# A hybrid decoder layer on one core: spills of y in four pieces, a second pool of slots, the diagonals of 1/rms earlier, and h of the second half on VectorE

## The chip, the core and the metric

The kernel runs on one core of a Trainium2 chip. The core has TensorE (PE in the profile; PEld is its weight load), VectorE (DVE), ScalarE (ACT), GpSimd (POOL) and SyncE (SP), which issues the transfers between memory and the on-chip SBUF. Matmuls write PSUM; VectorE and ScalarE read it, GpSimd doesn't. The metric is device time in microseconds (us) for one execution.

## The reference, cut to what matters

```
h = rmsnorm(x, g_pre) * (1 + scale) + shift        # x: 2048 tokens x 1024
proj = h @ w_in                                    # 7 groups of 512 columns
gu, gv, gg, rq, rk, rv, rg = split(proj)
y_gmlp = gu * (tril(w_s) LN(gv) + b) * silu(gg)    # 4 groups of 128 columns
y_ret = groupnorm(retention(rot(rq), rot(rk), rv)) * silu(rg)   # 4 heads of 128
y = concat(y_gmlp, y_ret)                          # 2048 x 1024
x + gate * rmsnorm(y @ w_out, g_post)
```

Everything is float32. `scale`, `shift` and `gate` come from a small matmul of `c` ahead of the rest.

## The kernel before, in words

**Tokens.** They are worked in two halves of 1024, each of two quads of 512 tokens. Activations lie transposed: 128 features in the partitions, tokens along the row. A tile of 128x512 float32 is 256 KB, 2 KB in each partition, and is the unit of nearly all work. Such tiles come from one pool, `big`, of 80 slots, handed out by `slot`; a new tile of it waits until the readers of the slot's last tile are done.

**Products.** A float32 product is three matmuls of 128x512 in a reduced format, high by high, low by high and high by low. Each operand is split for it: ScalarE writes the high part (`wh`, `hh`, `yh`), VectorE the rest (`wl`, `hl`, `yl`), one tile at a time.

**Stages of a half.** First the projections of v, q and k for retention (`token_unit`, 8 ticks of three matmuls for a chunk of 128 tokens), then v of the gMLP, then six *units* r0, r1, g0, u0, g1, u1 (numbers 0 to 5): two by two blocks of the gates and of u, each done with seven Strassen-Winograd products of four ticks instead of eight. VectorE adds the products up (`u`, `c`, line 783) out of PSUM, and the results multiply into y (`used`, lines 757 to 773): yR for retention, yT for the gMLP. y of a half is written to memory (`yspill`) and read back (`ya`) in the output stage at the end, which again pairs tokens for Strassen (`ys` are its sums) and multiplies by `w_out`, whose blocks are `or`. Weights of the units are loaded as `ur` and combined on GpSimd (`ut`).

**What sets the order.** PE, DVE, ACT and POOL run in the order in which the program emits the work, and `slots` is a hand-written timetable of it: `slots.at(t, fn)` puts a step t ticks ahead. `pump()` splits the next block of weights; how many run in each product of a unit is in EXTRA_PUMPS. SP's order is made by a scheduler from the same program.

**h of the second half.** `hbuild` makes the 16 tiles of h for tokens 1024 to 2047 (8 feature blocks, two quads) while the first half's units run. It needs `rb`, a row of 1/rms for each quad, spread over the partitions: `xdiag2` splits 4 columns of 1/rms (`rsh`, `rsl`) and makes eight 128x128 diagonals (`dgr`) on VectorE, and `xrow` multiplies them by ones on TensorE. BUILD tells at which tick of which unit this happens ("diag", "row", "x" for the load, "h" for a tile); the second quad's eight tiles are built from line 1139 on, where the second half's v projection starts (the *seam*).

Of the kernel before, what the change touches and what calls it, by code (L numbers as in the profile page):

```python
# [11 lines left out]
F32 = mybir.dt.float32  # L12
# [24 lines left out]
QK_PUMPS = ((), (), (1,), (1,), (1,), (1,), (1, 4), (1, 4))  # L37
EXTRA_PUMPS = {(0, 5): (0, 0, 0, 1, 1, 1, 2), (1, 4): (0, 1, 0, 1, 0, 1, 1), (1, 5): (0, 1, 1, 1, 1, 1, 1)}
SLOTS = 80
# [5 lines left out]
            ("B22", "S4"))  # L45
BUILD = {3: ((2, "diag", 0), (14, "row", 0), (20, "x", 0), (21, "x", 1)),
# [3 lines left out]
RV_PUMPS = ((1,),) * 7 + ((1, 4),)  # L50
# [48 lines left out]
def tile_hybrid_layer(ctx: ExitStack, tc, x, xt, wm, wg, win, wun, wout, wst, cols, rows, pos, cst,  # L99
# [39 lines left out]

    def slot(name, shape=(512,), dtype=F32):  # L140
        return big.tile([P, *shape], dtype, name=name, tag="s")


    raw, blocks = {}, {}
# [176 lines left out]
    def hnew(half, q, kb):  # L321
        hi, lo = slot("hh", dtype=F32R), slot("hl", dtype=F32R)
        hT[half, q, kb] = (hi, lo)
        return hi, lo
# [93 lines left out]
    def v_small(half, ch, ps, when=(0, 1, 7, 12, 14)):  # L418
# [28 lines left out]
        def into_y():  # L447
            y = yT[half, ch // QUAD]
            for g in range(GROUPS):
                V.scalar_tensor_tensor(y[:, ch % QUAD, g, :], box["mx"][:, g, :],  # L450
                                       cols_t[:, 32 + g:33 + g], bs_b[:, g, :], ALU.mult, ALU.add)
# [17 lines left out]
    def ret_pair(pool, half, pr_, ch, ps, delay=0):  # L469
# [99 lines left out]
        def into_y():  # L569
            for i in range(2):  # L570
                h = h0 + i
                S.activation(yR[half, ch // QUAD][:, :, h, :], box["ytp", i], AF.Copy,
                             scale=cols_t[:, 36 + h:37 + h])
# [10 lines left out]

    def yspill(half, part):
        for ch in range(NCH):
            t = yd[half, ch, part] = ydram.tile([P, 4, P], F32, name=f"yd{half}{ch}{part}")
            SP.dma_start(t, (yR, yT)[part][half, ch // QUAD][:, ch % QUAD, :, :])


    def pair_loads(half, ch):
        a = {}

        def load():
            for m in range(2):
                for part in range(2):
                    t = a[f"A{m + 1}{part + 1}"] = slot("ya", (4, P))
                    SP.dma_start(t, yd[half, ch + QUAD * m, part])

        return a, load  # L600
# [156 lines left out]
    def used(half, kind, pair, up, c, q, nj, in_psum):  # L757
        y = (yR if kind == "r" else yT)[half, q][:, :, 2 * pair + nj, :]
        c3 = c.rearrange("p (c t) -> p c t", c=QUAD)

        def times(eng, by):
            eng.tensor_tensor(y, y, by, ALU.mult)  # L762

        if kind == "u":
            slots.at(0, lambda: times(V if in_psum else G, c3))
            return

        def gate():
            g = up.tile([P, QUAD, P], F32, name="sg", tag="k", bufs=6) if in_psum else c3
            S.activation(g, c3, AF.Silu)  # L770
            slots.at(1, lambda: times(G, g))

        slots.at(0, gate)
# [317 lines left out]

    areas = []

    def opened(name):
        areas.append(tc.tile_pool(name=name, bufs=1, reuse_waits="tile"))
        return areas[-1].__enter__()

    def closed(n=1):
        for _ in range(n):
            areas.pop().__exit__(None, None, None)  # L1100

    def y_tiles(name, half, to):
        pool = opened(f"{name}{half}")
        for q in range(2):
            to[half, q] = pool.tile([P, QUAD, 4, P], F32, name=f"{name}{half}{q}")

# [11 lines left out]
    def build1(q, kb):  # L1118
        n = q * KB + kb
        hbuild(1, q, kb, hb["x"].pop(0), hb[q], kb % 2 == 1 if q else kb in (1, 7), (3, 5), True)  # L1120
        if n + 2 < 2 * KB:
            fetch1(n + 2)

    qk = {}
    for half in range(2):

        if half == 0:
            with tc.tile_pool(name="start", bufs=1, reuse_waits="tile") as sp:
                first = start(sp)
            y_tiles("yR", half, yR)  # L1130
            rp = opened(f"ret{half}")
# [4 lines left out]
        for ch in range(QUAD if half == 0 else 0, NCH):  # L1136
            if half == 1 and ch == 0:
                for n in range(KB):
                    slots.at(6 + 3 * n, partial(build1, 1, n))
                slots.at(4, partial(yspill, 0, 1))  # L1140
            ps = token_unit(half, 0, ch, "prv", () if half == 0 else RV_PUMPS[ch])
            rv_small(half, ch, ps)
            if half == 1 and ch == 2:
                closed(3)
                y_tiles("yR", half, yR)
                rp = opened(f"ret{half}")
                for n, fn in enumerate(tables(half, rp)):
                    slots.at(n + 2, fn)
# [20 lines left out]
        for ch in range(NCH):  # L1169
            if ch == 2:  # L1170
                closed()
                y_tiles("yT", half, yT)
                up = opened(f"unit{half}")
# [9 lines left out]
        for un in range(len(UNITS)):  # L1183
# [3 lines left out]
            if un == 2:  # L1187
                slots.at(4, partial(yspill, half, 0))
            if half == 0 and un in BUILD:
# [12 lines left out]

    slots.at(3, partial(yspill, 1, 1))
    pools = []
# [75 lines left out]
```

## Time and profile before

| | |
|---|---|
| median of 3 runs | 907.1 us (906.3 to 907.86) |
| the profiled execution | 906.63 us, span 904.9 us |
| TensorE busy | 850.8 us (94%) |
| VectorE busy | 663.7 us (73%) |
| GpSimd busy | 415.5 us (46%) |
| ScalarE busy | 319.8 us (35%) |
| transfers | 100.60 MB, mean 111 GB/s |

The span is from the first to the last instruction; 1.7 us of the execution lie around it. Busy shares are averages over stages with different limits. The granted clock of TensorE is given as a share of 2.4 GHz, so 0.50 is 1.2 GHz.

### The profile page before, as it was taken

To read this page: it belongs to the slowest core of one execution; us is meant where nothing else is said; L and a number is where in the kernel's file an instruction comes from. 1 tells how busy PE (TensorE), PEld (TensorE's weight loads), DVE (VectorE), ACT (ScalarE), POOL (GpSimd) and SP (SyncE) were. 2 spreads that over 40 slices of the span, in tenths; PEclk is the share of its full clock that TensorE was granted. 3 is DMA by queue.
4 is the path that set the end of the run, shared out by engine and by line. 5 is a ranking of instruction groups with operands and counts; after the bars stand their busy time and mean duration, and the time that the engine had idled before them with its cause. 6 is when DMAs were issued, how large, how long until landed. Compare 5 with 4: busy or idle time off the path is not lost.

```text
span 904.9 us, 11859 instructions
## 1 busy us (share of the span) xinstructions
PE 850.8 (94%) x4074; PEld 698.6 (77%) x4074; DVE 663.7 (73%) x1242; ACT 319.8 (35%) x621; POOL 415.5 (46%) x448
## 2 busy tenths in 40 slices
PE   2999999999999995999999999999999968899996
PEld 1778888888888884777888888888888746678885
DVE  4989876567984648779886665897356797887776
ACT  4673223323453334451111221354423343433341
POOL 2040363355756556130334334675548663545451
PEclk9999999999999998999999999999999979999999
DMA  8961331300021422463232100011331844364432
GB/s 324 330 238 37 92 117 59 103 14 1 8 87 47 163 70 70 129 231 129 81 94 94 59 1 1 1 47 47 138 83 49 291 149 177 112 222 178 140 141 93
DMA packets 49597, 100.60 MB, mean 111 GB/s; under 512 B 5888, under 2 KB 6016, under 8 KB 49536
## 3 DMA queue, kind: packets, MB, share of 16 engines
q1 hardware_dynamic: 49536, 99.83, 32.9%
q8 instruction: 32, 0.52, 0.2%
q14 instruction: 29, 0.24, 0.1%
HBM read 83.03 MB, written 16.78 MB: 110 GB/s over the span
## 4 chain that ended last, share of the span: by engine, by line
PE 77%; DVE 10%; DMA 6%; issue 4%; ACT 2%; POOL 1%; SPq 0%; DVEq 0%; ACTq 0%; POOLq 0%
PE pqk L241 6%; PE pqk L239 6%; PE pqk L240 5%; PE pY L241 3%; PE pY L239 3%; PE pY L240 3%; PE pv L241 3%; PE pv L240 3%; PE pv L239 3%; DVE wl L187 2%; PE pX L239 2%; PE pX L240 2%; PE pX L241 2%; PE pZ L239 2%; PE pZ L241 2%
## 5 line engine op out<-in xcount | busy, mean ns | idle before, releaser
L239 PE MATMUL pqk<-wh,hh 128*128 128x512 f32 x240 | 102.3, 426 | 0.0
L502 POOL TENSOR_TENSOR rA<-rA,rB 128x512 f32<-128x512 f32 x32 | 42.5, 1327 | 118.9 <-DVE rB L494 84.8
L241 PE MATMUL pqk<-wh,hl 128*128 128x512 f32 x240 | 94.7, 395 | 0.0
L240 PE MATMUL pqk<-wl,hh 128*128 128x512 f32 x240 | 93.7, 390 | 0.0
L516 ACT COPY qkT<-tp 128x512 f32<-128x512 f32 x32 | 18.8, 586 | 155.6 <-PE tp L507 155.6
L187 DVE TENSOR_TENSOR wl<-wr,wh 128x512 fp32r<-128x512 f32 x62 | 63.9, 1045 | 1.9 <-ACT wh L184 1.7
L762 POOL TENSOR_TENSOR yT<-yT,c 128x512 f32<-128x512 f32 x24 | 37.2, 1556 | 60.7 <-DVE c L783 43.0
L241 PEld LDWEIGHTS pqk<-wh,hl 128*128 128x128 f32 x240 | 45.0, 188 | 10.4
L239 PE MATMUL pv<-wh,hh 128*128 128x512 f32 x128 | 51.9, 406 | 0.0
L240 PEld LDWEIGHTS pqk<-wl,hh 128*128 128x128 f32 x240 | 45.5, 189 | 6.8 <-issue 0.2
L239 PEld LDWEIGHTS pqk<-wh,hh 128*128 128x128 f32 x240 | 45.4, 189 | 6.4 <-issue 0.2
L241 PE MATMUL pv<-wh,hl 128*128 128x512 f32 x128 | 50.1, 391 | 0.0
L240 PE MATMUL pv<-wl,hh 128*128 128x512 f32 x128 | 50.0, 390 | 0.0
L783 DVE TENSOR_TENSOR u<-pY,s 128x512 f32<-128x512 f32 x24 | 16.5, 688 | 42.7 <-PE pY L241 25.3
L241 PE MATMUL pY<-sh,wl 128*128 128x512 f32 x96 | 38.6, 402 | 9.5 <-DVE wl L187 9.5
L184 ACT CAST wh<-ut 128x512 fp32r<-128x512 f32 x48 | 28.7, 620 | 47.7 <-POOL ut L224 47.6
L241 PE MATMUL zY<-wh,yl 128*128 128x512 f32 x96 | 38.4, 400 | 3.0 <-DVE yl L618 2.9
L439 ACT ACTIVATE vh<-pv,nbv,rsv 128x128 f32<-128x128 f32 x64 | 24.1, 456 | 47.4 <-POOL nbv L434 47.4
L560 DVE TENSOR_SCALAR yq<-o,gmv,grs 128x128 f32<-128x128 f32 x64 | 23.3, 405 | 23.8 <-POOL grs L553 23.8
L672 POOL TENSOR_SCALAR zrs<-zss 128x1 f32<-128x1 f32 x16 | 18.2, 1139 | 47.5 <-ACT jz L665 46.9
L239 PE MATMUL zY<-wh,yh 128*128 128x512 f32 x96 | 38.1, 397 | 2.0 <-DVE u L668 1.1
L492 DVE TENSOR_TENSOR rA<-pqk,cos_t 128x512 f32<-128x512 f32 x28 | 19.2, 687 | 28.1 <-PE pqk L241 28.1
(251 smaller groups left out, 2641.8 us busy)
## 6 DMA issues: line engine op xcount, KB each, us to landing
wr<-in_win SPq DMA_DIRECT2D x64, 256.0 KB, 3.5
ur<-in_wun SPq DMA_DIRECT2D x48, 256.0 KB, 3.1
slab<-in_wm SPq DMA_DIRECT2D x16, 512.0 KB, 6.4
ya<-yd SPq DMA_DIRECT2D x32, 256.0 KB, 3.9
xr<-in_x SPq DMA_DIRECT2D x16, 512.0 KB, 4.6
out<-xr SPq DMA_DIRECT2D x32, 256.0 KB, 2.2
or<-in_wout SPq DMA_DIRECT2D x28, 256.0 KB, 5.3
xt<-in_xt SPq DMA_DIRECT2D x24, 256.0 KB, 4.8
```

The costliest lines, as they stand in the source:

```text
L184: S.copy(hi, r)
L187: eng.tensor_tensor(lo, r, hi.bitcast(F32), ALU.subtract)
L239: T.matmul(ps, l[0], r[0], start=first, stop=False, skip_group_check=reopened)
L240: T.matmul(ps, l[0], r[1], start=False, stop=False, skip_group_check=reopened)
L241: T.matmul(ps, l[1], r[0], start=False, stop=last, skip_group_check=reopened)
L439: S.activation(vh[:, g, :], ps[:, g * P:(g + 1) * P], AF.Identity, bias=nb[:, g:g + 1], scale=rs[:, g:g + 1])
L492: V.tensor_tensor(A, ps.rearrange("p (g d) -> p g d", g=8), tab["cos"][:, ch, :].unsqueeze(1).broadcast_to([P, 8, 64]), ALU.mult)
L502: G.tensor_tensor(A, A, box["B"].rearrange("p g h d -> p (g h d)"), ALU.add)
L516: S.copy(qkT, box["tp"])
L560: V.tensor_scalar(yq[h][:, ch % QUAD, :], box["o"][:, i, :], mv[:, i, 0:1], rs[:, i:i + 1], ALU.subtract, ALU.mult)
L672: G.tensor_scalar(r, ss[:, m, 0:1], ss[:, m, 1:2], EPS, ALU.add, ALU.add)
L762: eng.tensor_tensor(y, y, by, ALU.mult)
```

## The change

1. EXTRA_PUMPS: in the second half four more blocks of weights are split in units 3 to 5, ahead of the output stage (35 for 31); in the first half the 19 of units 4 and 5 are spread otherwise.
2. BUILD: both diagonals and rows are made in unit 2 (they were in units 3 and 5), the eight h tiles of the first quad in units 3, 4 and 5 (they were in 4 and 5), and those of the second quad start at tick 1 of the seam, not 6.
3. `build1`: all 16 h tiles are built with two VectorE instructions and one ScalarE instruction. Ten of them took one GpSimd, two ScalarE and one VectorE instruction before.
4. y of a half is no longer one tile for a quad but eight tiles of 2 KB. yR of the first half has a pool of its own (`ys`, 8 slots), which the first four blocks of h of the second half then use; yR of the second half lies in `big`, which frees its slots after its spill.
5. `yspill` writes one column group (one head or group) of one quad with one transfer, 512 pieces of 512 bytes, where it wrote one chunk of 128 tokens in 128 pieces of 2 KB. The number of transfers stays. yT leaves in two pieces, columns 0 and 1 in unit 4, columns 2 and 3 at the end, where all of it left at the end.
6. `used`: the last unit of the second half multiplies three results into yT on VectorE, which did it on GpSimd.

```diff
@@ -35,7 +35,8 @@
 SUMS_G = ((), (), (0, 5), (4, 6), (5, 7), (5, 7), (), ())
 V_PUMPS = ((),) * 7 + ((1, 4),)
 QK_PUMPS = ((), (), (1,), (1,), (1,), (1,), (1, 4), (1, 4))
-EXTRA_PUMPS = {(0, 5): (0, 0, 0, 1, 1, 1, 2), (1, 4): (0, 1, 0, 1, 0, 1, 1), (1, 5): (0, 1, 1, 1, 1, 1, 1)}
+EXTRA_PUMPS = {(0, 4): (0, 0, 0, 0, 0, 1, 1), (0, 5): (0, 0, 0, 1, 0, 1, 1), (1, 3): (0, 0, 0, 1, 0, 1, 1),
+               (1, 4): (1, 1, 0, 1, 1, 1, 1), (1, 5): (1, 0, 1, 0, 1, 1, 1)}
 SLOTS = 80
 TOKEN_PASSES = 4
 R_WHEN = (0, 2, 5, 6, 8, 9, 10, 11, 12, 14, 15, 16)
@@ -43,10 +44,10 @@
 GROUP = {"u": 0, "g": 2, "r": 6}
 PRODUCTS = (("B11", "A11"), ("T2", "S2"), ("B21", "A12"), ("T3", "S3"), ("T1", "S1"), ("T4", "A22"),
             ("B22", "S4"))
-BUILD = {3: ((2, "diag", 0), (14, "row", 0), (20, "x", 0), (21, "x", 1)),
-         4: ((14, "h", 0, 0), (22, "h", 0, 1)),
-         5: ((0, "diag", 1), (3, "h", 0, 2), (7, "h", 0, 3), (11, "h", 0, 4), (14, "row", 1),
-             (15, "h", 0, 5), (19, "h", 0, 6), (23, "h", 0, 7))}
+BUILD = {2: ((1, "diag", 0), (8, "row", 0), (12, "diag", 1), (19, "row", 1), (20, "x", 0), (21, "x", 1)),
+         3: ((5, "h", 0, 0), (18, "h", 0, 1)),
+         4: ((3, "h", 0, 2), (12, "h", 0, 3), (21, "h", 0, 4)),
+         5: ((3, "h", 0, 5), (12, "h", 0, 6), (20, "h", 0, 7))}
 RV_PUMPS = ((1,),) * 7 + ((1, 4),)
 GROUPS_OUT = (2, 1, 1, 1, 1, 1, 1)
 EPS = 1e-6
@@ -137,9 +138,21 @@
     invf_b = const.tile([P, 64], F32, name="invf_b")
     tab = {}
 
-    def slot(name, shape=(512,), dtype=F32):
-        return big.tile([P, *shape], dtype, name=name, tag="s")
-
+    def slot(name, shape=(512,), dtype=F32, pool=None):
+        return (pool or big).tile([P, *shape], dtype, name=name, tag="s")
+
+
+    areas, opens = [], []
+
+    def opened(name, bufs=1):
+        opens.append(tc.tile_pool(name=name, bufs=bufs, reuse_waits="tile"))
+        areas.append(opens[-1].__enter__())
+        return areas[-1]
+
+    def closed(n=1):
+        for _ in range(n):
+            areas.pop()
+            opens.pop().__exit__(None, None, None)
 
     raw, blocks = {}, {}
     IN_BLOCKS = TOKEN_PASSES * KB
@@ -319,7 +332,8 @@
         return t
 
     def hnew(half, q, kb):
-        hi, lo = slot("hh", dtype=F32R), slot("hl", dtype=F32R)
+        pool = areas[0] if half == 1 and q == 0 and kb < 4 else None
+        hi, lo = slot("hh", dtype=F32R, pool=pool), slot("hl", dtype=F32R, pool=pool)
         hT[half, q, kb] = (hi, lo)
         return hi, lo
 
...
@@ -569,7 +583,9 @@
         def into_y():
             for i in range(2):
                 h = h0 + i
-                S.activation(yR[half, ch // QUAD][:, :, h, :], box["ytp", i], AF.Copy,
+                y = slot("yR", (QUAD, P), pool=None if half else areas[0])
+                yR.setdefault((half, ch // QUAD), {})[h] = y
+                S.activation(y, box["ytp", i], AF.Copy,
                              scale=cols_t[:, 36 + h:37 + h])
 
         steps = [rotate, added, turn, turned, score, causal, outp, stats, root, norm]
@@ -582,10 +598,12 @@
     ydram = ctx.enter_context(tc.tile_pool(name="ydram", bufs=1, space=bass.MemoryType.DRAM))
     yd = {}
 
-    def yspill(half, part):
-        for ch in range(NCH):
-            t = yd[half, ch, part] = ydram.tile([P, 4, P], F32, name=f"yd{half}{ch}{part}")
-            SP.dma_start(t, (yR, yT)[part][half, ch // QUAD][:, ch % QUAD, :, :])
+    def yspill(half, part, cols):
+        for q in range(2):
+            if (half, part, q) not in yd:
+                yd[half, part, q] = ydram.tile([P, QUAD, 4, P], F32, name=f"yd{half}{part}{q}")
+            for n in cols:
+                SP.dma_start(yd[half, part, q][:, :, n, :], (yR, yT)[part][half, q][n])
 
 
     def pair_loads(half, ch):
...
@@ -755,14 +773,14 @@
         return on_v, on_g, late
 
     def used(half, kind, pair, up, c, q, nj, in_psum):
-        y = (yR if kind == "r" else yT)[half, q][:, :, 2 * pair + nj, :]
+        y = (yR if kind == "r" else yT)[half, q][2 * pair + nj]
         c3 = c.rearrange("p (c t) -> p c t", c=QUAD)
 
         def times(eng, by):
             eng.tensor_tensor(y, y, by, ALU.mult)
 
         if kind == "u":
-            slots.at(0, lambda: times(V if in_psum else G, c3))
+            slots.at(0, lambda: times(V if in_psum or (half == 1 and pair == 1) else G, c3))
             return
 
         def gate():
...
@@ -1117,7 +1127,7 @@
 
     def build1(q, kb):
         n = q * KB + kb
-        hbuild(1, q, kb, hb["x"].pop(0), hb[q], kb % 2 == 1 if q else kb in (1, 7), (3, 5), True)
+        hbuild(1, q, kb, hb["x"].pop(0), hb[q], True, (3, 5))
         if n + 2 < 2 * KB:
             fetch1(n + 2)
 
@@ -1127,7 +1137,7 @@
         if half == 0:
             with tc.tile_pool(name="start", bufs=1, reuse_waits="tile") as sp:
                 first = start(sp)
-            y_tiles("yR", half, yR)
+            opened("ys", 8)
             rp = opened(f"ret{half}")
             table_inputs()
             qk = second_quad(rp, *first)
@@ -1136,13 +1146,12 @@
         for ch in range(QUAD if half == 0 else 0, NCH):
             if half == 1 and ch == 0:
                 for n in range(KB):
-                    slots.at(6 + 3 * n, partial(build1, 1, n))
-                slots.at(4, partial(yspill, 0, 1))
+                    slots.at(1 + 3 * n, partial(build1, 1, n))
+                slots.at(10, partial(yspill, 0, 1, (2, 3)))
             ps = token_unit(half, 0, ch, "prv", () if half == 0 else RV_PUMPS[ch])
             rv_small(half, ch, ps)
             if half == 1 and ch == 2:
-                closed(3)
-                y_tiles("yR", half, yR)
+                closed(2)
                 rp = opened(f"ret{half}")
                 for n, fn in enumerate(tables(half, rp)):
                     slots.at(n + 2, fn)
...
@@ -1185,7 +1194,9 @@
                 for n, fn in enumerate(late):
                     slots.at(1 + 3 * (n // 2) + n % 2, fn)
             if un == 2:
-                slots.at(4, partial(yspill, half, 0))
+                slots.at(5, partial(yspill, half, 0, range(HEADS)))
+            if un == 4:
+                slots.at(6, partial(yspill, half, 1, (0, 1)))
             if half == 0 and un in BUILD:
                 for t, what, *args in BUILD[un]:
                     slots.at(t, partial({"diag": diag1, "row": row1, "x": fetch1, "h": build1}[what],
@@ -1200,7 +1211,7 @@
                 prepare(groups[0], len(PRODUCTS) * 4)
             unit(half, un, up)
 
-    slots.at(3, partial(yspill, 1, 1))
+    slots.at(3, partial(yspill, 1, 1, (2, 3)))
     pools = []
 
     def begin():
```

VectorE's instructions at the first product of unit 2 of the first half, before the change (`c` is the last sum of unit 1; `wl<-ut` is the low part of T2, the weights of this product; `u` is its sum):

```order
L783 TENSOR_TENSOR c_2956<-pY,s_2850 128x512
L783 TENSOR_TENSOR c_2980<-pZ,u_2869 128x512
L187 TENSOR_TENSOR wl<-ut,wh 128x512
L187 TENSOR_TENSOR wl<-ur,wh 128x512
L783 TENSOR_TENSOR u_3037<-pY,s_3018 128x512
L187 TENSOR_TENSOR wl<-ut,wh 128x512 x2
L783 TENSOR_TENSOR u_3085<-pY,s_3018 128x512
```

And with the change, from the same sum on:

```order
L801 TENSOR_TENSOR c_2992<-pZ,u_2881 128x512
L294 CAST rsh<-rs_85 128x4
L295 TENSOR_TENSOR rsl<-rs_85,rsh 128x4
L298 TENSOR_SCALAR dgr<-cst_t,rsh 128x128
L299 TENSOR_SCALAR dgr<-cst_t,rsl 128x128
...
L299 TENSOR_SCALAR dgr<-cst_t,rsl 128x128
L200 TENSOR_TENSOR wl<-ut,wh 128x512
L200 TENSOR_TENSOR wl<-ur,wh 128x512
L801 TENSOR_TENSOR u_3062<-pY,s_3028 128x512
L200 TENSOR_TENSOR wl<-ut,wh 128x512 x2
L294 CAST rsh<-rs_85 128x4
L295 TENSOR_TENSOR rsl<-rs_85,rsh 128x4
```

The conversion of 1/rms and the eight diagonals, which stood like this ahead of `wl` at the first product of unit 5, now stand there in unit 2, and the second set follows `wl` for the next two blocks.

VectorE from the first sum of the last unit of the second half to the first low part of y (`yl`) of the output stage, before (`or<-or` are sums of output weights):

```order
L783 TENSOR_TENSOR u_6861<-pY,s_6823 128x512
L187 TENSOR_TENSOR wl<-or,wh 128x512 x2
L762 TENSOR_TENSOR yT_5512<-yT_5512,pX 128x4x128
L203 TENSOR_TENSOR or<-or 128x512
L783 TENSOR_TENSOR u_6930<-pY,s_6823 128x512
L203 TENSOR_TENSOR or<-or 128x512
L187 TENSOR_TENSOR wl<-or,wh 128x512 x2
L203 TENSOR_TENSOR or<-or 128x512
L783 TENSOR_TENSOR c_6964<-pZ,u_6930 128x512
L203 TENSOR_TENSOR or<-or 128x512
L187 TENSOR_TENSOR wl<-or,wh 128x512 x3
L618 TENSOR_TENSOR yl<-ya,yh 128x512
```

And with the change:

```order
L801 TENSOR_TENSOR u_6906<-pY,s_6870 128x512
L200 TENSOR_TENSOR wl<-or,wh 128x512 x2
L216 TENSOR_TENSOR or<-or 128x512
L780 TENSOR_TENSOR yT_5506<-yT_5506,pX 128x512
L200 TENSOR_TENSOR wl<-or,wh 128x512 x2
L801 TENSOR_TENSOR u_6965<-pY,s_6870 128x512
L200 TENSOR_TENSOR wl<-or,wh 128x512 x2
L801 TENSOR_TENSOR c_6989<-pZ,u_6965 128x512
L780 TENSOR_TENSOR yT_5509<-yT_5509,c_6989 128x512
L200 TENSOR_TENSOR wl<-or,wh 128x512 x2
L636 TENSOR_TENSOR yl<-ya,yh 128x512
```

Seven `wl<-or` and four sums `or<-or` stood in that stretch, and now eight and one; one multiplication into yT is new in it, and two more follow it. Ahead of the stretch three `or<-or` and six `wl<-or` now stand, where two `wl<-or` stood.

SP's transfers at the start of the output stage, before (`yd<-yT` is the spill, `xr` are rows of x for the residual):

```order
L598 DMA ya<-yd_3759 128x512
L176 DMA or<-in_wout 128x512 x7
L588 DMA yd_7070<-yT_5513 128x512
L588 DMA yd_7072<-yT_5513 128x512
L588 DMA yd_7074<-yT_5513 128x512
L588 DMA yd_7076<-yT_5513 128x512
L588 DMA yd_7062<-yT_5512 128x512
L588 DMA yd_7064<-yT_5512 128x512
L588 DMA yd_7066<-yT_5512 128x512
L588 DMA yd_7068<-yT_5512 128x512
L696 DMA xr<-in_x 128x1024 x4
L176 DMA or<-in_wout 128x512 x8
```

And with the change:

```order
L616 DMA ya<-yd_3397 128x512
L606 DMA yd_6681<-yT_5506 512x1x128
L606 DMA yd_6684<-yT_5509 512x1x128
L606 DMA yd_6684<-yT_5507 512x1x128
L606 DMA yd_6681<-yT_5508 512x1x128
L714 DMA xr<-in_x 128x1024 x2
L189 DMA or<-in_wout 128x512 x2
L714 DMA xr<-in_x 128x1024 x2
L189 DMA or<-in_wout 128x512 x6
```

Four spills stand where eight stood, two of the rows of x come later, and the `or` that followed the rows now follow in two pieces; 20 `or` stand ahead of these rows, 18 of them in one run, where 20 stood in runs of 7, 6 and 7.

## Rows read from the trace of the kernel before

**Rows 1.** The page: each engine's busy us, share of the span, instructions.

```profile
PE 850.8 (94%) x4074; PEld 698.6 (77%) x4074; DVE 663.7 (73%) x1242; ACT 319.8 (35%) x621; POOL 415.5 (46%) x448
```

**Rows 2.** The waits of TensorE: line, releaser, us in total, times, longest.

```profile
PE pY L241 <- DVE wl L187: 9.5, 1, 9.5
PE zX L241 <- DVE yl L618: 6.5, 4, 5.5
PE zY L241 <- DVE yl L618: 2.9, 2, 2.0
...
PE prv L241 <- DVE hl L346: 1.2, 1, 1.2
...
PE prv L240 <- DVE wl L187: 0.8, 1, 0.8
```

**Rows 3.** Timeline of TensorE in unit 5: start, us, instruction, idle time before it.

```profile
349.77 0.39 PE L239 MATMUL pY<-sh,wh 128*128 128x512 f32 x1
349.99 0.39 PE L240 MATMUL pY<-sl,wh 128*128 128x512 f32 x1
359.86 0.80 PE L241 MATMUL pY<-sh,wl 128*128 128x512 f32 x1 [9.47 <-DVE wl L187]
```

**Rows 4.** Timeline of VectorE in the same stretch of unit 5.

```profile
347.93 1.22 DVE L281 CAST rsh<-rs 128x4 fp32r<-128x4 f32 x1
...
359.12 0.68 DVE L187 TENSOR_TENSOR wl<-ut,wh 128x512 fp32r<-128x512 f32 x1
```

**Rows 5.** Windows after three stalls: TensorE busy us (instructions), PEclk, DMA share, GB/s.

```profile
359.80:365.10 5.30, 5.24 (x13) 0.51 0.13 42
729.60:733.80 4.20, 4.12 (x10) 0.52 0.09 33
742.80:747.40 4.60, 4.56 (x13) 0.63 0.96 349
720.40:723.40 3.00, 3.00 (x12) 1.00 0.16 59
```

**Rows 6.** Timeline of VectorE, then of TensorE, at unit 2's first product.

```profile
289.36 0.69 DVE L783 TENSOR_TENSOR c<-pZ,u 128x512 f32<-128x512 f32 x1 [2.10 <-PE pZ L241]
292.26 0.39 PE L241 MATMUL pY<-sh,wl 128*128 128x512 f32 x1
```

**Rows 7.** Timeline of GpSimd at the same place.

```profile
290.97 1.77 POOL L762 TENSOR_TENSOR yR<-yR,c 128x512 f32<-128x512 f32 x1 [0.53 <-ACT c L770]
...
293.95 1.30 POOL L224 TENSOR_TENSOR ut<-ur,ut 128x512 f32<-128x512 f32 x1
298.12 1.30 POOL L762 TENSOR_TENSOR yT<-yT,sg 128x512 f32<-128x512 f32 x1 [2.88 <-ACT sg L770]
```

**Rows 8.** Timeline of VectorE at unit 3's diagonals.

```profile
314.48 0.28 DVE L285 TENSOR_SCALAR dgr<-cst_t,rsh 128x128 fp32r<-128x128 f32 x1
314.67 0.28 DVE L286 TENSOR_SCALAR dgr<-cst_t,rsl 128x128 fp32r<-128x128 f32 x1
```

**Rows 9.** Timeline of VectorE at the start of the output stage.

```profile
723.33 1.75 DVE L203 TENSOR_TENSOR or<-or 128x512 f32<-128x512 f32 x1 [2.99 <-POOL or L202]
725.00 3.43 DVE L187 TENSOR_TENSOR wl<-or,wh 128x512 fp32r<-128x512 f32 x2
```

**Rows 10.** Timeline of TensorE there.

```profile
720.40 0.50 PE L239 MATMUL pZ<-sh,wh 128*128 128x512 f32 x1 [2.01 <-DVE c L783]
...
729.68 0.80 PE L241 MATMUL zX<-wh,yl 128*128 128x512 f32 x1 [5.52 <-DVE yl L618]
```

**Rows 11.** Windows: busy us (instructions) of PE, PEld, DVE, ACT, POOL; PEclk, DMA share, GB/s.

```profile
680.00:700.00 20.00, 20.00 (x90) 16.57 (x89) 13.30 (x16) 7.82 (x14) 16.45 (x12) 1.00 0.15 40
700.00:730.00 30.00, 22.45 (x97) 17.68 (x96) 24.71 (x25) 11.18 (x20) 20.62 (x15) 0.95 0.64 219
730.00:765.00 35.00, 30.22 (x112) 22.75 (x112) 30.88 (x36) 15.10 (x30) 18.93 (x12) 0.90 0.58 211
```

**Rows 12.** The tile xt: instructions, ns min/median/max, first and last start.

```profile
L330 DVE SCALAR_TENSOR_TENSOR xt<-xt,a_col,rb x10: 739/744/1882, 63.1 to 403.5; 128x512 f32<-128x512 f32 x10
```

More of the change, by code (lines that the diff above doesn't have):

```diff
@@ L449, in into_y @@
             for g in range(GROUPS):
-                V.scalar_tensor_tensor(y[:, ch % QUAD, g, :], box["mx"][:, g, :],
+                V.scalar_tensor_tensor(y[g][:, ch % QUAD, :], box["mx"][:, g, :],
                                        cols_t[:, 32 + g:33 + g], bs_b[:, g, :], ALU.mult, ALU.add)
@@ L597, in load @@
                     t = a[f"A{m + 1}{part + 1}"] = slot("ya", (4, P))
-                    SP.dma_start(t, yd[half, ch + QUAD * m, part])
+                    SP.dma_start(t, yd[half, part, m][:, ch, :, :])
         return a, load
@@ L1090, in prepare, with y_tiles @@
                 slots.at(at + t, fn)
[L1092 to L1103, printed above, removed]
+    def y_tiles(half):
+        pool = opened(f"yT{half}")
+        tiles = {(g, q): pool.tile([P, QUAD, P], F32, name=f"yT{half}{q}{g}") for g in range(GROUPS)
+                 for q in range(2)}
         for q in range(2):
-            to[half, q] = pool.tile([P, QUAD, 4, P], F32, name=f"{name}{half}{q}")
+            yT[half, q] = [tiles[g, q] for g in range(GROUPS)]
     hb = {"x": []}
@@ L1171, in tile_hybrid_layer @@
                 closed()
-                y_tiles("yT", half, yT)
+                y_tiles(half)
                 up = opened(f"unit{half}")
```

## The prediction

> **What bounds the kernel now.** I read the page first: TensorE is busy 850.8 us, 94% of the span [rows 1], so only what makes it wait, or run at half clock, can be won. The list of its waits comes next [rows 2]. Setting aside the start, two places stand out: one wait of 9.5 us in unit 5 for `wl`, and a dozen in the output stage, the largest 5.5 and twice 2.0 us [rows 2, 10], nearly all for VectorE. Two small ones, 0.8 and 1.2 us, lie in the seam. Then I read the timelines at these places.
>
> In unit 5 TensorE stops after 349.99 and goes on at 359.86 [rows 3]. VectorE shows why: from 347.93 to 359.12 it converts 1/rms and makes eight diagonals, and only then the `wl` that TensorE waits for [rows 4]. These ten tiny instructions take 11.2 us, 1.12 each. In unit 3 the same diagonals come at a pitch of 0.20 us (314.48 to 314.67) [rows 8]. In unit 5 GpSimd ran back to back beside them, in unit 3 it had stopped. So in this trace a VectorE instruction that works in SBUF gets its turn only between two of GpSimd's.
>
> The stalls cost more than their length. After the wait of 9.47 us the granted clock was 0.51 for 5.3 us, 1.2 GHz: 13 matmuls that need 13 × 0.227 = 3.0 at the full-speed pitch (0.22 to 0.23 between starts, as at 349.77 and 349.99 [rows 3]). The loss is 2.3. After 5.52 us it was 4.2 for 10, so 1.9, and after 2.05 us 4.6 for 13, so 1.6; the wait of 2.01 us was followed by full clock [rows 5].
>
> In the output stage VectorE is busy 24.7 of 30 and 30.9 of 35 us, while GpSimd is busy 20.6 and 18.9 [rows 11]. TensorE waits until 720.40 for the sum `c`; and `yl`, for which it waits until 729.68, stands behind a sum of output weights that itself waited 2.99 us for GpSimd, and behind weight splits of 3.43 us for two [rows 9, 10].
>
> **What the change does, part by part.** The sum is made against the profiled execution, 906.63 us, 0.5 below the median.
>
> *Diagonals out of unit 5.* The block of ten no longer stands ahead of that `wl`, and the h tiles on that path are spread out. The stall of 9.47 and its slow clock of 2.3 go: −11.8. The first h tiles are ready earlier, and the second quad's start five ticks sooner (five ticks of three matmuls, 3.4 us at 0.227). That covers the seam's 1.2 us for `hl` and most likely the 0.8 for `wl`: −2.0, bound from below by nothing.
>
> *Diagonals into unit 2.* The order shows the same block in the same position, ahead of `wl<-ut` of the first product. So the question is not whether it delays TensorE, but how long it takes there. It starts when `c` ends, 289.36 + 0.69 = 290.05; TensorE needs the `wl` at 292.26 [rows 6]. GpSimd has just three instructions there, from 290.97 to 293.95 + 1.30, after 0.53 us of idle time, and then 2.88 us of nothing until 298.12 [rows 7]. In the idle 0.53 us two or three of the ten fit at 0.20; three more go in turn with GpSimd's three, which end near 290.97 + 3 × 1.3 = 294.9; the other four take 0.8, to 295.7, and `wl` 0.68 more, to 296.4. Stall: 296.4 − 292.26 = 4.1. From below it is 290.05 + 10 × 0.20 + 0.68 − 292.26 = 0.5, from above unit 5's pace, 290.05 + 11.2 + 0.68 − 292.26 = 9.7. For the clock I take the 1.7 between those after 5.52 and 2.05 us; bounds 0 and 2.3. Together +5.8. The second block stands after the next `wl` pair, in a stretch where GpSimd is idle until 298.12, and its followers feed no product that is due: nothing, and at unit 5's pace some 5 us of stall that I keep for the rival.
>
> *h on VectorE.* Ten tiles cost GpSimd 1.3 us less each and VectorE one instruction of 0.74 more each [rows 12]; 7.4 us of VectorE over units 3 to 5 and the seam, where it has slack and GpSimd now less to hold it with. I cost it at nothing; what hides it is that the `wl` of the next product stands ahead of the tiles. Without that cover it is the third rival.
>
> *Four blocks more before the output stage.* They lie in units 3 to 5 of the second half. VectorE is busy 13.3 of 20 us at 680 to 700 [rows 11], so four splits at 0.7 to 1.7 us and the earlier sums fit barely; I take +0.7 for a wait that this may open (0 to 1.4).
>
> *Output stage.* With `or` loaded in one run ahead of y's reads, the sums `or<-or` come earlier and `c` finds VectorE free: −2.0, the whole wait. Between that `c` and the first `yl`, a sum that waited 2.99, three splits and the `yl` become one multiplication, two splits and the `yl`. `c` can end at about 718.4 (2.0 before 720.40); the four then take 0.68 × 4 = 2.7 alone, up to 5.9 with 1.7 for those beside GpSimd. TensorE would want `yl` 2.01 sooner than 729.68 − 5.52 = 724.16, at 722.15. So 721.1 to 724.3: a wait of 0 to 2.1. I take 0.5: −5.0, and −1.9 of clock. Fourteen of the first group's 28 output splits are then done instead of nine, which leaves VectorE some five instructions less for what follows; of the next wait of 2.05 and its 1.6 of clock I count half: −1.8. The other waits up to 812 us I leave.
>
> *Spills.* The same number, in shorter pieces. yT's first half has left long before; SP waits at the end for four multiplications on VectorE that follow their sums at once, where it waited for GpSimd's. That brings the last `or` loads some microseconds sooner, and it is not in the sum. Nothing reads these spills for tens of microseconds.
>
> The sum: −11.8 − 2.0 + 5.8 = −8.0 in the first half; +0.7 − 2.0 − 6.9 − 1.8 = −10.0 in the output stage. 906.6 − 18.0 = 888.6, and with the median's 0.5, **889 us**.
>
> **Rivals.**
>
> *The block in unit 2 runs at unit 5's pace.* For it: there each of ten took 1.12 us on average [rows 4]. Against: three GpSimd instructions can't hold back ten [rows 7]. It would need GpSimd's next work to slide beside the block. Price: stall 9.7 + clock 2.3 = 12.0 for 5.8, so 6.2 more: 895 us.
>
> *The output stage stays bound by VectorE.* For it: it was busy 30.9 of 35 us from 730 on [rows 11], and a wait removed at 720 may come back at 740. Then only 3 us of the 10 stay: 896 us. Against: five splits and the wait for GpSimd's sums really leave the stretch. Both of these together: 902 us.
>
> *Slower: h tiles hold up the weights.* A two-input instruction on VectorE took 1.88 us at worst for 0.74 [rows 12], 1.14 more, as turns with GpSimd cost it. Ten moved tiles are twenty such instructions in units 3 to 5 and the seam. If each stood ahead of a `wl` that TensorE awaits, that is 22.8: 889 + 22.8 = 912 us. It decides from 18/1.14 = 16 of the twenty on. Against: the median of the ten that ran there is 0.74, so most found GpSimd idle, and GpSimd loses ten instructions of 1.3 us at just these places. The Trainium skill, "SBUF — State Buffer", section "Who interferes with whom", has a rule that speaks for this rival: a VectorE instruction with two inputs in SBUF contends with a GpSimd instruction that reads SBUF, and the one that comes second is blocked for the whole instruction. By that rule each of the twenty that meets GpSimd pays; the trace agrees on the worst case (1882 ns) and bounds how often it comes by the median (744 ns).
>
> **How the numbers follow.** A change under 0.2% (1.8 us) can't be told from none with this kernel. Chances: the forecast 0.58, with its own range 883 to 896 (the unit 2 stall from 3 to 5.5 with clock 0 to 2.3, the output stage from −4 to −13); the block at the old pace 0.12; the output stage unmoved 0.18; both 0.04; the h tiles 0.08, of which a part ends within 0.2%. The middle two lie at 895 and 896. For the range I leave out 912, half of 902, and below what no bound reaches: 881 to 900 us. Faster 0.89, same 0.03, slower 0.08.
>
> **What would show it.** Right: no wait of over 1 us in unit 5; in unit 2 one wait of 3 to 5.5 us for `wl` at the first product, with eight `dgr` ahead of it on VectorE, some at 0.2 and some at 1.2 us; no wait for `c` and under 2 us for `yl` at the start of the output stage, with a granted clock of 1.0 there; the second half's units 3 to 5 without waits over 1.5 us. Wrong: waits for `wl` spread over units 3 to 5 of the first half beside `xt` or `hl` of over 1.5 us, a stall of 9 us in unit 2, or VectorE still waiting for GpSimd's sums ahead of the first `yl`. If `ya` or `or` land later than their readers want them, the transfers in shorter pieces are the cause that I left out.

## The result, and the profile after

The changed kernel takes 897.2 us (median); the ratio to the kernel before is 0.989, 95% interval 0.9871 to 0.991. It is faster by 9.5 us (the kernel before has a median of 906.7 in four executions), inside the range of 881 to 900, above the forecast's own range of 883 to 896, and half of the 18 that the sum gave. One of the four executions of the changed kernel took 1225.8 us at a granted clock of 0.66 and is left out of the ratio. The page's busy times come first, then TensorE's waits (those at the start left out):

```profile
span 895.4 us, 11883 instructions
PE 851.6 (95%) x4074; PEld 701.0 (78%) x4074; DVE 668.7 (75%) x1255; ACT 312.0 (35%) x611; POOL 402.8 (45%) x435
```

```profile
PE pY L252 <- DVE u L801: 6.0, 1, 6.0
PE pY L254 <- DVE wl L200: 3.6, 1, 3.6
PE zY L254 <- DVE yl L636: 2.9, 2, 2.1
...
PE zX L254 <- DVE yl L636: 1.8, 2, 1.5
PE zX L252 <- ACT yh L635: 1.3, 1, 1.3
PE zY L252 <- DVE u L686: 1.1, 1, 1.1
```

Set beside [rows 2], the wait of 9.5 us in unit 5 and the two in the seam are gone; 3.6 us in unit 2 stand in their place. The 5.5 and 2.0 us at the start of the output stage are gone too, but a wait of 6.0 us for `u` is new. It lies at 709 us, in the last unit, where nothing waited before.

VectorE at the first product of unit 2, the place of [rows 6]:

```profile
289.71 0.50 DVE L294 CAST rsh<-rs 128x4 fp32r<-128x4 f32 x1
...
290.52 0.28 DVE L299 TENSOR_SCALAR dgr<-cst_t,rsl 128x128 fp32r<-128x128 f32 x1
290.72 1.36 DVE L298 TENSOR_SCALAR dgr<-cst_t,rsh 128x128 fp32r<-128x128 f32 x1
292.00 1.29 DVE L299 TENSOR_SCALAR dgr<-cst_t,rsl 128x128 fp32r<-128x128 f32 x1
293.22 1.30 DVE L298 TENSOR_SCALAR dgr<-cst_t,rsh 128x128 fp32r<-128x128 f32 x1
294.44 0.27 DVE L299 TENSOR_SCALAR dgr<-cst_t,rsl 128x128 fp32r<-128x128 f32 x1
...
295.03 0.68 DVE L200 TENSOR_TENSOR wl<-ut,wh 128x512 fp32r<-128x512 f32 x1
```

Three of the ten take 1.3 us each, one turn for each of GpSimd's three instructions; the others take 0.2 to 0.5. VectorE at the new wait, and then windows of TensorE after the three longest waits (length, busy, instructions, granted clock, DMA share, GB/s):

```profile
698.65 1.77 DVE L216 TENSOR_TENSOR or<-or 128x512 f32<-128x512 f32 x1 [1.95 <-POOL or L215]
701.61 1.76 DVE L216 TENSOR_TENSOR or<-or 128x512 f32<-128x512 f32 x1 [1.19 <-POOL or L215]
703.29 3.42 DVE L200 TENSOR_TENSOR wl<-or,wh 128x512 fp32r<-128x512 f32 x2
706.63 1.74 DVE L216 TENSOR_TENSOR or<-or 128x512 f32<-128x512 f32 x1
708.30 0.68 DVE L801 TENSOR_TENSOR u<-pY,s 128x512 f32<-128x512 f32 x1
```

```profile
295.70:302.10 6.40, 6.34 (x15) 0.51 0.28 105
709.00:714.60 5.60, 5.57 (x13) 0.50 0.42 146
746.00:749.60 3.60, 3.51 (x9) 0.57 0.00 0
```

Before the change all four sums of output weights stood behind the first `u` of the last unit, the fourth just ahead of `yl` [rows 9]. With four blocks split earlier three of them stand ahead of that `u`, with two splits between them. Between the end of the last `c` (696.70) and `u` VectorE waits 3.1 us for GpSimd in two places and spends 5.3 us on the three sums and 3.4 on the two splits, some 1.7 us apiece beside GpSimd.

The windows have 15, 13 and 9 matmuls of 0.227 us at full speed, so the slow clock costs 3.0, 2.7 and 1.5 us. The wait ahead of it doesn't settle how long it lasts. Run e5 below is the same program up to unit 2, has the same wait there (3.60 us), and then nine slow matmuls instead of 15, a loss of 1.7 us:

```profile
296.00:299.70 3.70, 3.67 (x9) 0.55 0.45 172
```

In the eight traces that have this wait the loss is 1.6 to 3.0 us, and the changed kernel itself, run again as e11, loses 3.0 after its wait of 2.11 us, where it lost 1.5 here.

The output weights' last loads also hold VectorE up. GpSimd's timeline, which sums them first, and VectorE's:

```profile
735.62 2.51 POOL L220 TENSOR_TENSOR or<-or 128x512 f32<-128x512 f32 x2 [14.46 <-DMA or<-in_wout]
737.60 1.09 DVE L200 TENSOR_TENSOR wl<-or,wh 128x512 fp32r<-128x512 f32 x1 [5.40 <-ACT wh L197]
```

In the kernel before GpSimd had them at 750.37. They land sooner now, but VectorE, which has done more of the output splits by then, is idle for 5.4 us until they are there.

**The ledger.** First half: −9.5 − 2.3 − 0.8 − 1.2 + 3.6 + 3.0 = −7.2. The start of one product shows that this is about all of it. It is the product that now waits for `u`, before and with the change:

```profile
710.07 0.39 PE L239 MATMUL pY<-sh,wh 128*128 128x512 f32 x1
709.03 0.79 PE L252 MATMUL pY<-sh,wh 128*128 128x512 f32 x1 [6.05 <-DVE u L801]
```

TensorE is there at 709.03 − 6.05 = 702.98 for 710.07, so 7.1 us are won by then, and from there to the end only 2.4 of the span's 904.9 − 895.4 = 9.5. At the start of the output stage it is −2.0 − 5.5 − 1.9 + 6.05 + 2.7 = −0.7; from 730 to 812 us the waits and the slow clock behind them came to 9.5 us before and come to 8.9 now. The last 1 us or so stands in no wait of these lists.

### The profile page after: what moved, and what is told of

It is laid out like the page before. It is cut to its first block, busy times and chain, and to the rows that moved or that the text cites. A ratio compares the mean times of both kernels' runs of the same rounds, so it can differ in the third digit from the quotient of the medians.

```text
span 895.4 us, 11883 instructions
## 1 busy us (share of the span) xinstructions
PE 851.6 (95%) x4074; PEld 701.0 (78%) x4074; DVE 668.7 (75%) x1255; ACT 312.0 (35%) x611; POOL 402.8 (45%) x435
## 4 chain that ended last, share of the span: by engine, by line
PE 82%; DVE 7%; issue 4%; ACT 2%; DMA 2%; POOL 2%; SPq 0%; DVEq 0%; ACTq 0%; POOLq 0%
PE pqk L254 6%; PE pqk L252 6%; PE pqk L253 6%; PE pY L254 4%; PE pY L252 4%; PE pY L253 3%; PE pv L252 3%; PE pv L254 3%; PE pv L253 3%; PE prv L253 2%; PE prv L252 2%; PE prv L254 2%; PE pX L253 2%; PE pX L252 2%; PE pZ L252 2%
## 5 line engine op out<-in xcount | busy, mean ns | idle before, releaser
L780 POOL TENSOR_TENSOR yT<-yT,c 128x512 f32<-128x512 f32 x21 | 33.3, 1590 | 44.0 <-DVE c L801 23.8
L252 PE MATMUL pY<-sh,wh 128*128 128x512 f32 x96 | 39.7, 414 | 6.0 <-DVE u L801 6.0
L200 DVE TENSOR_TENSOR wl<-ut,wh 128x512 fp32r<-128x512 f32 x48 | 43.3, 919 | 1.8 <-ACT wh L197 1.7
```

Source lines behind the costliest of these rows:

```text
L200: eng.tensor_tensor(lo, r, hi.bitcast(F32), ALU.subtract)
L252: T.matmul(ps, l[0], r[0], start=first, stop=False, skip_group_check=reopened)
```

## The experiments

The changed kernel, run once more beside e9 and e10 (e11 below), gave 0.9903 for 0.989; so ratios that differ by less than about 0.002 are not read, and the traces decide there.

**e1, diagonals behind the splits.**

```diff
-BUILD = {2: ((1, "diag", 0), (8, "row", 0), (12, "diag", 1), (19, "row", 1), (20, "x", 0), (21, "x", 1)),
-         3: ((5, "h", 0, 0), (18, "h", 0, 1)),
+BUILD = {2: ((12, "diag", 0), (19, "row", 0), (20, "x", 0), (21, "x", 1)),
+         3: ((5, "h", 0, 0), (12, "diag", 1), (18, "h", 0, 1), (19, "row", 1)),
```

> The changed kernel with both blocks of diagonals behind the weight splits: the first at tick 12 of unit 2, the second at tick 12 of unit 3. Theory A (the place in VectorE's queue makes the stall): at tick 12 the block stands behind the `wl` that TensorE awaits and beside an idle GpSimd, so the wait of 3.6 us in unit 2 and its slow clock of 1.6 us go, and no other comes: 5.2 us less than the changed kernel, 892.0 us. Rival (the ten instructions cost VectorE's time wherever they stand): a wait of 2 us or more turns up for another VectorE result in unit 2 or 3, and the time stays within 2 us of 897.2.

891.75 us, 0.9844 (0.983 to 0.9857). The wait of 3.6 us is gone and no other came. VectorE's timeline there:

```profile
296.66 0.16 DVE L294 CAST rsh<-rs 128x4 fp32r<-128x4 f32 x1
...
298.31 1.41 DVE L299 TENSOR_SCALAR dgr<-cst_t,rsl 128x128 fp32r<-128x128 f32 x1
300.23 0.69 DVE L801 TENSOR_TENSOR u<-pY,s 128x512 f32<-128x512 f32 x1 [0.52 <-PE pY L254]
```

Nine of the ten fit into 1.7 us, the tenth takes a turn, and `u` still finds VectorE idle. By the ratios 4.2 to 5.3 us are won, about the 5.2 expected. Theory A holds: the place made the stall. The new place differs in two things, though: it lies behind the `wl`, and GpSimd is idle there. The next run has the first without the second.

**e4, the kernel before with the second block alone moved.**

```diff
-         5: ((0, "diag", 1), (3, "h", 0, 2), (7, "h", 0, 3), (11, "h", 0, 4), (14, "row", 1),
+         5: ((3, "h", 0, 2), (7, "h", 0, 3), (11, "h", 0, 4), (12, "diag", 1),
-             (15, "h", 0, 5), (19, "h", 0, 6), (23, "h", 0, 7))}
+             (15, "h", 0, 5), (19, "h", 0, 6), (20, "row", 1), (23, "h", 0, 7))}
```

> The kernel before with one move alone: its second block of diagonals at tick 12 of unit 5 for tick 0, and its row at tick 20. Theory A: the wait of 9.47 us and its slow clock of 2.3 us go, and nothing else changes: 11.8 us less than before, 895 us, as good as the whole change. Rival (GpSimd's h tiles make the ten instructions slow at any place in unit 5): the block of 11 us then delays the sums `u` and `c` and the splits of the next products, and at least 4 us of waits come back: 899 us or more.

899.1 us, 0.9922 (0.991 to 0.9934): the rival's side by a hair. VectorE's block and TensorE's waits:

```profile
357.55 1.26 DVE L281 CAST rsh<-rs 128x4 fp32r<-128x4 f32 x1
...
362.47 0.27 DVE L286 TENSOR_SCALAR dgr<-cst_t,rsl 128x128 fp32r<-128x128 f32 x1
```

```profile
362.60 0.73 PE L304 MATMUL rb_ps<-dgr,ones 128*128 128x512 f32 x2 [1.33 <-DVE dgr L285]
365.89 0.47 PE L239 MATMUL pY<-hh,wh 128*128 128x512 f32 x1 [2.56 <-DVE u L783]
```

The block takes 5.1 us for 11.2, since GpSimd works beside its first three instructions only (1.2 to 1.4 us each), but that is enough: 4.1 us of waits come back, with 1.7 us of slow clock. A place behind the splits does not suffice where GpSimd is at work. Even so, one move of one block has seven to eight tenths of what the whole change gives. The seam's two waits are gone here too, though h still starts at tick 6 and on GpSimd.

**e5, h on the engines of before.**

```diff
-        hbuild(1, q, kb, hb["x"].pop(0), hb[q], True, (3, 5))
+        hbuild(1, q, kb, hb["x"].pop(0), hb[q], kb % 2 == 1 if q else kb in (1, 7), (3, 5), True)
```

> The changed kernel with the h tiles of the second half on the engines of before (ten of sixteen multiply on GpSimd, two ScalarE instructions, one VectorE instruction). Theory A (the prediction: h on VectorE costs and gives nothing, since the weight splits stand ahead of it): no wait over 1.5 us comes in units 3 to 5 or the seam, and the time is within 1 us of the changed kernel's ratio of 0.989. Rival (GpSimd's ten multiplications take VectorE's turns from the splits): waits of 2 us or more in all come back there, and the ratio is 0.991 or more.

898.2 us, 0.9909 (0.9895 to 0.9922), between the two expectations and not to be told from the changed kernel's 0.989 and 0.9903. TensorE's timeline has three small waits around the end of unit 4, the first and the last of which are

```profile
342.36 0.47 PE L252 MATMUL pY<-sh,wh 128*128 128x512 f32 x1 [0.39 <-DVE u L801]
...
349.72 0.50 PE L254 MATMUL pY<-hh,wl 128*128 128x512 f32 x1 [0.60 <-DVE wl L200]
```

With the third, 0.29, they make 1.3 us. The changed kernel has none there. So by the traces h on VectorE gives some 1 us of waits and costs none; the times can't show it.

**e6, the split counts of before.**

```diff
-EXTRA_PUMPS = {..., (1, 3): (0, 0, 0, 1, 0, 1, 1),
-               (1, 4): (1, 1, 0, 1, 1, 1, 1), (1, 5): (1, 0, 1, 0, 1, 1, 1)}
+EXTRA_PUMPS = {..., (1, 4): (0, 1, 0, 1, 0, 1, 1), (1, 5): (0, 1, 1, 1, 1, 1, 1)}
```

> The changed kernel with the split counts of before in the second half (31 in units 3 to 5 for 35). Theory A (the four earlier blocks moved the sums `or<-or` ahead of the first `u` of the last unit, and thereby opened the wait of 6.05 us): that wait goes, and one for `c` or `yl` comes back at the start of the output stage as before, 2.0 and up to 5.5 us; the time is within 2 us of the changed kernel's, that is, this part gives nothing or little by itself. Rival B (the four blocks relieve the output stage): without them the waits after the start of the output stage grow by 3 us or more and the ratio rises to 0.992 or more.

894.95 us, 0.9872 (0.9857 to 0.9886). The 6.05 us are gone, as theory A has it, and TensorE waits 1.0 us for `c` and, longer than the 5.5 expected, for `yl` instead, behind splits beside GpSimd's sums of y (VectorE, then TensorE):

```profile
714.42 1.76 DVE L216 TENSOR_TENSOR or<-or 128x512 f32<-128x512 f32 x1 [2.83 <-POOL or L215]
...
717.77 5.10 DVE L200 TENSOR_TENSOR wl<-or,wh 128x512 fp32r<-128x512 f32 x3
```

```profile
723.53 0.79 PE L254 MATMUL zX<-wh,yl 128*128 128x512 f32 x1 [8.28 <-DVE yl L636]
```

So the four earlier blocks give nothing: the same work stalls TensorE in one place or the other. The spills and loads are those of the change here, and the two waits at the start of the output stage are no shorter than before it (1.0 and 8.3 us for 2.0 and 5.5); it was the split counts that took them away.

**e2, the sums later in the queue.**

```diff
-            slots.at(3, lambda: V.tensor_tensor(t2, t3, t2, ALU.add))
-            slots.at(4, lambda: split(i, t2, eng, gap))
+            slots.at(6, lambda: V.tensor_tensor(t2, t3, t2, ALU.add))
+            slots.at(7, lambda: split(i, t2, eng, gap))
```

> The changed kernel with VectorE's sum of output weights (`or<-or`, line 216) and the split after it three ticks later. Theory A (order): the new wait of 6.05 us for `u` at 709 comes because four such sums, which wait for GpSimd, and two splits between them stand ahead of `u` in VectorE's queue. With two sums and no split ahead of it, the wait falls under 1.5 us and its slow clock of 2.6 us goes: 6 to 8 us less, 889 to 891 us. Rival B (VectorE simply has more work there than time): the wait comes back at the next `u` or `c` or at `yl`, and the time is within 2 us of 897.2.

895.2 us, 0.9876 (0.9861 to 0.9891): rival B. (Ahead of the first `u` stood three sums and two splits, by the rows above, not four and two.) The wait moved to the next `u`, 6.0 us in all for 6.05:

```profile
703.85 0.50 PE L252 MATMUL pY<-sh,wh 128*128 128x512 f32 x1 [1.05 <-DVE u L801]
714.58 0.80 PE L252 MATMUL pY<-hh,wh 128*128 128x512 f32 x1 [4.95 <-DVE u L801]
```

**e7, the whole sums on VectorE.**

```diff
-            G.tensor_tensor(t3, t3, t1, ALU.subtract)
-            G.tensor_tensor(t1, t1, t2, ALU.subtract)
-            slots.at(3, lambda: V.tensor_tensor(t2, t3, t2, ALU.add))
+            def sums():
+                V.tensor_tensor(t3, t3, t1, ALU.subtract)
+                V.tensor_tensor(t1, t1, t2, ALU.subtract)
+                V.tensor_tensor(t2, t3, t2, ALU.add)
+            slots.at(3, sums)
```

> The changed kernel with the two GpSimd subtractions of each of the four sums of output weights done on VectorE too, so that VectorE has eight instructions more and GpSimd eight less. Theory D (the turns: beside a busy GpSimd each VectorE instruction waits up to 1.1 us, so a sum costs VectorE more in waits than the whole sum done by itself at 0.6 each): the wait of 6.05 us for `u` falls to under 2 us, its slow clock goes, and 5 to 8 us are won; ratio 0.981 to 0.984. Rival B (VectorE lacks time there): eight instructions of 0.6 to 0.7 us more make the waits there longer by up to 5 us; ratio 0.989 to 0.995.

893.3 us, 0.986 (0.9846 to 0.9873), between the two expectations and nearer to theory D's. VectorE's timeline:

```profile
698.78 0.68 DVE L216 TENSOR_TENSOR or<-or 128x512 f32<-128x512 f32 x1
699.49 0.69 DVE L217 TENSOR_TENSOR or<-or 128x512 f32<-128x512 f32 x1
700.22 0.69 DVE L218 TENSOR_TENSOR or<-or 128x512 f32<-128x512 f32 x1
...
704.32 0.68 DVE L805 TENSOR_TENSOR u<-pY,s 128x512 f32<-128x512 f32 x1
```

A whole sum takes 2.1 us here, where its last third alone took 1.7 and waited for the rest. With eight instructions more VectorE reaches `u` 4.0 us sooner (704.3 for 708.3). TensorE itself was 0.9 us ahead there, as its slow clock in unit 2 was shorter this time; its wait shrinks by the other 3.1, to 2.94 us. The slow clock behind it cost 1.7 us for 2.7, but 3.0 in e8 and 1.7 in e12, which have the same wait; that part can't be put down to the edit.

**e3, the rows of x three products later.**

```diff
+            if n == 3:
                 for m in range(2):
                     xr.append(pools[0].tile([P, D], F32, name="xr", tag="x", bufs=4))
```

> The changed kernel with the loads of the rows of x (`xr`, 512 KB each) issued three products later in each group of the output stage, so that the last output weights `or` don't queue behind four of them. Theory C (transfers): GpSimd waits 14.5 us for those `or` until 735.6, VectorE is idle for 5.4 us behind it, and the waits of 7.3 us in all from 736 to 752 with 1.7 us of slow clock follow from it. The `or` then land 2.5 to 5 us sooner, and 3 to 5 us are won: 892 to 894 us. Rival: the spills ahead of them set the landing, or VectorE is the limit anyway, and the time is within 1.5 us of 897.2.

894.5 us, 0.9875 (0.986 to 0.989). GpSimd's wait shrinks from 14.5 to 11.7 us, and TensorE's waits from 736 to 752 us from 6.0 to 4.5. The sign is theory C's, the size 1.4 to 2.5 us by the ratios, which is hardly clear of their spread, and 1.5 by the waits, for 3 to 5: the weights' splits then run beside GpSimd. Part of the landing is the rival's. In the changed kernel SP can issue the last spill, behind which rows and weights stand, only when VectorE's last multiplication into yT is done (VectorE, then SP):

```profile
726.69 0.69 DVE L780 TENSOR_TENSOR yT<-yT,c 128x512 f32<-128x512 f32 x1
727.41 0.51 SPq L606 DMA_DIRECT2D yd<-yT  x1
```

No run moves that spill behind the loads.

**e8, e1, e7 and e3 together.**

> The changed kernel with three edits together: the diagonals behind the splits (tick 12 of units 2 and 3), the sums of output weights on VectorE, the rows of x three products later. If theory A, C and D hold and the parts add up: 4.1 us for the first as measured, 5 to 8 for the sums, 1 to 2 for the rows: 10 to 14 us less than the changed kernel, ratio 0.974 to 0.978. If the sums come out as rival B has it, 3 to 5 us less, ratio 0.984 to 0.986.

885.3 us, 0.9775 (0.9761 to 0.9788): the parts add up at the low end.

**e9, e8 with e2's delays.**

> The three edits of the run before, and the sums of output weights and their splits three ticks later too (six sums on VectorE ahead of the first `u` of the last unit, where nine and two splits stood). Theory D with order: the wait of 2.94 us for `u` falls under 1 us; the twelve instructions ahead of the next `u` take 0.6 to 0.7 us each beside an idle GpSimd, some 8 us, about what TensorE leaves them, so at most 1 us comes back there. 2 to 3 us less than the three edits: ratio 0.974 to 0.976. Rival B (VectorE lacks time): the wait moves to the second `u` in full, ratio 0.977 to 0.979.

886.0 us, 0.9778 (0.9763 to 0.9793): rival B, the wait of 2.94 us became one of 4.17 at the second `u`. With GpSimd all but out of the way (one sum of y runs beside a split), VectorE has just more to do there than TensorE leaves time for; order only moves the wait.

**e10, the last unit's multiplications on GpSimd.**

```diff
-            slots.at(0, lambda: times(V if in_psum or (half == 1 and pair == 1) else G, c3))
+            slots.at(0, lambda: times(V if in_psum else G, c3))
```

> The changed kernel with the last unit's three multiplications into yT on GpSimd again. Theory A (GpSimd's instruction costs VectorE a turn of 1.1 us, the multiplication on VectorE 0.6): the waits for `yl` at the start of the output stage grow by 1 to 3 us and the last spills come later; ratio 0.990 to 0.992. Rival (VectorE's three instructions cost as much as they save): the ratio stays at 0.989 or falls by 0.001.

897.4 us, 0.9904 (0.989 to 0.9918). One wait for `yl` of 0.75 us is new, less than theory A's 1 to 3; the time is that of the changed kernel on the same chip (e11).

**e11, the changed kernel again.**

> The changed kernel itself once more, beside the other runs on the same chip: ratio 0.988 to 0.990, the same waits as before (3.6 us in unit 2, 6.05 us for `u`). If it lies at 0.987 or below, the differences of 0.002 to the other runs are not to be read.

897.9 us, 0.9903 (0.9886 to 0.992), just above the range expected, with the same waits of 3.60 and 6.06 us.

**e12, e8 with the four last subtractions on VectorE.**

```diff
-            G.tensor_tensor(t, t, kept.pop(("T2", kb)), ALU.subtract)
+            t2 = kept.pop(("T2", kb))
+            slots.at(2, lambda: V.tensor_tensor(t, t, t2, ALU.subtract))
```

> The three edits together, and the four last subtractions of output weights (for the product T4) on VectorE too instead of GpSimd. Theory D (turns): GpSimd then has only the sums of y beside VectorE from 724 on, the splits there fall from 1.1 to 1.8 us to 0.6, and the waits of 4.5 us from 728 to 736 shrink to 1.5 us or less; ratio 0.973 to 0.975 for 0.9775. Theory C (the landing of `or` at 724 sets it): VectorE now waits itself for that landing, ahead of `yl` and `u`, nothing is won or a wait of 1 to 3 us is added; ratio 0.977 to 0.981.

882.4 us, 0.9744 (0.9731 to 0.9757), the best of all. VectorE waits for the load itself, and then runs at its own pace:

```profile
723.92 0.69 DVE L225 TENSOR_TENSOR or<-or 128x512 f32<-128x512 f32 x1 [1.35 <-DMA or<-in_wout]
...
726.34 0.69 DVE L200 TENSOR_TENSOR wl<-or,wh 128x512 fp32r<-128x512 f32 x1
```

TensorE's waits that answer to the 4.5 us of e8 are 0.2, 0.6 and 1.5 us, 2.3 for the 1.5 expected: theory D's side, by half. In e8 GpSimd's subtractions began at 724.0, as VectorE's do at 723.9 here:

```profile
724.02 2.54 POOL L224 TENSOR_TENSOR or<-or 128x512 f32<-128x512 f32 x2 [12.34 <-DMA or<-in_wout]
```

So the 2.2 us won are not the landing's but come from what followed it, beside GpSimd. What the other 2.3 hang on is not shown.

## Why the prediction was right, and where its sum was wrong

**First half: right.** −7.2 for −8.0. The stall in unit 2 was 3.6 for 4.1, the pace of the block as counted: seven instructions at idle pace, three in turn with GpSimd. e1 shows the cause, by taking it away. The slow clock behind it was mis-sized: 3.0 for 1.7, outside its bounds of 0 to 2.3. I had taken it from two other stalls, and the runs show that even the same wait in the same place leaves it open, at 1.6 to 3.0.

**The seam: right in size, wrong in reason.** The 2.0 came, but e4 has them without the earlier start; they went with the stall of unit 5.

**h on VectorE: nearly right.** Costed at nothing, worth some 1 us by e5's waits. The slower rival did not happen: of the sixteen tiles made there on VectorE three took 1.8 us, and TensorE waited for none. Its argument from [rows 12] was weaker than it looked, for four of those ten ran at 63 to 73 us, far from the place.

**Output stage: the step that failed** is "four splits at 0.7 to 1.7 us and the earlier sums fit barely; I take +0.7 for a wait that this may open (0 to 1.4)". It measured 6.05 and 2.7 of clock. I counted the splits and let the sums leave the stretch ahead of `c` and `yl` for nothing, though the text on the order says that three of them now stand ahead of it, and so ahead of `u`, each behind two of GpSimd's. The gain of 2.0 and 6.9 at `c` and `yl` did come, and e6 shows that it is the same debt paid one product sooner. The 1.8 counted at the next wait did not come. The last loads of `or` landed sooner, as I had said (735.6 for 750.4), but VectorE now wanted them sooner still; e3 and e12 took 1.5 and 2.2 us of waits away there.

**The number.** The last unit and the output stage gave 2.4 us for 10.0. That is near the price of the rival "the output stage stays bound by VectorE" (896 us, to which I gave 0.18), but not its way: the wait came back at 709, ahead of the stage, and not at 740, and at 737 VectorE had been idle, waiting for loads. The time lies in the range of 881 to 900 because of the room given to the rivals, not because the sum was right. Of the signs of being right all came but the last: 6.05 us in the second half's unit 5, where 1.5 was the most.

**Spills:** the pieces of 512 bytes land as fast as those of 2 KB, in a median of 2.6 and 2.8 us for 2.8 and 2.8. Reading y back took 5.2 us in the median for 3.9, at other places of the schedule; ScalarE waited 0.4 us in all for it, for 8.9 before. No run takes back the spills, the eight tiles of y or the second pool by themselves; what they are worth is not shown.

## What to carry to other kernels

When work is moved ahead of a stretch that stalls, look for the first instruction that someone awaits behind its new place, in the same queue, and count the waits that the moved work brings with it; otherwise the stall moves too. Where VectorE and GpSimd both work in SBUF, a small VectorE instruction costs a whole GpSimd instruction (0.16 to 0.28 us alone, 1.2 to 1.4 beside it): put such blocks where GpSimd is idle, and weigh giving GpSimd's part of a sum to VectorE even where VectorE is the one that is awaited (e7, e12). Carry the slow clock behind a stall as a range, and read a difference of 1 us or so between two profiles only after taking it out.

## What the runs showed that I had not expected

Twelve instructions taken from GpSimd and put on VectorE, the engine that TensorE awaits, made the kernel faster, 0.9744 against 0.9844 with the diagonals alone moved (of that, the later rows of x had 1.4 to 2.5 us by themselves). An instruction of 0.16 us alone (`rsh` in e1) took 1.26 us beside GpSimd (e4).
